# FFN units on inputs that carry the row factor, convolution taps read from PSUM, and 2 KB tiles placed at 0 modulo 128

## The chip, the cores and the metric

The kernel runs on one core of one Trainium2 chip. The metric is the device time of one launch in microseconds (us), the median of three timed runs; lower is better. Beside it stands one profiled execution, whose trace gives every duration below.

## The reference, cut to what matters

Two transformer-like blocks follow each other on 512 tokens of width 1024, in float32. The first ends with a feed-forward layer whose two halves pass through a causal convolution of three taps:

```
h2 = rms_norm(x, ffn_pre_g)                       # row factor r(token) and gain g(channel)
u  = h2 @ w_up                                    # (512, 8192)
c  = conv_w[0]*u[t-2] + conv_w[1]*u[t-1] + conv_w[2]*u[t] + conv_b
g, val = split(c)                                 # 4096 + 4096 columns
x  = x + rms_norm((gelu_tanh(g) * val) @ w_down, ffn_post_g)
```

The second block normalises x again and applies one input projection (query, index, gate, recurrence and merge columns), sparse attention over the 256 best keys, a linear recurrence, and output projections. Before the feed-forward layer the first block has a sliding-window and a differential attention.

## The kernel before, in words

**Layout.** Activations lie transposed: channels on the 128 partitions, 512 tokens along the free axis, so that a tile of 128 channels is 128 x 512 in float32, 2 KB per partition. A 1024-wide activation is eight such tiles (index k). Each is kept twice, as a high part rounded to float32r and the low rest (`xh`, `xl`). Weights are split likewise (`wh`, `wl`, or `sh`, `sl` in two halves when all four places for `wh` are taken). A product is then three matmuls (`mm3`, lines 534 to 546): xh with wh, xl with wh, xh with wl.

**Units.** One unit is 128 output channels: eight k times three matmuls, 24 matmuls of 512 columns into one PSUM buffer. The weights of one unit are 512 KB, fetched by SyncE into one of three `wr` buffers, copied to `wh` by ScalarE (`hi_w`, line 477) and subtracted into `wl` by VectorE or GpSimd (`lo_w`, line 495). `unit` (line 548) runs one unit. `group` (line 561) runs several, with `outer="k"` interleaved: for each k all units of the group. With `halves=True` it does the first 256 tokens of all units, then the others. Behind a unit stands its evacuation, a generator that reads PSUM.

**Order.** No engine's order is fixed by hand. While the program is built, a planner (`account`, line 288; `sched`, line 437; `until`, line 453) keeps a modelled time for each engine and lets a generator go on when its engine and data are ready in that model. What comes out is one fixed order per engine, and each engine works in that order and waits for semaphores. `vp` (line 357) puts a subtraction or product on VectorE or GpSimd, whichever the model has free first.

**PSUM.** Eight buffers of 128 x 512: two each of `mm`, `lg`, `pt`, `o`. `psm` (line 385) takes the buffer of a unit from the kinds in `self.mmt`. In the feed-forward layer that is `("mm",)`, two buffers.

**The boundary between stages** (`boundary`, line 1177) adds the normalised output to the residual `xres`, writes the next stage's `xh`, `xl` with the gain g but without the row factor r (which needs all channels), and computes r into `rbn` (two halves, `nx["rok"]`). So the next stage's matmuls start before r is known, and r is multiplied in when a unit's PSUM is evacuated.

**The feed-forward layer** (`ffn`, line 1219). ug0, uv0, ug1 run as a group in halves. Then uv1, ug2, uv2, ... each run as a unit; after every eight pairs come the eight `dn` units on `acth`, `actl`. The evacuation of an up unit (`conv`, line 1228) is: VectorE `u` = PSUM times r and release of the PSUM buffer; ScalarE `c` = u times tap 2 plus bias; VectorE twice `c` += u shifted by one (511 columns) and by two (510 columns) times a tap. Then ScalarE takes the gelu (gate half), or VectorE or GpSimd the product and ScalarE and VectorE the split into `acth`, `actl` (value half).

**The second block** (`block2`, line 1336) starts with ckv, kw, qi0 in halves and the group qi1, qi2, qi3 on unscaled inputs. Beside that group `rescale` (line 1405) computes, for each k that the group has read (`qk["k"]`), xres times gain times r into `xn` on VectorE, and `resplit` writes it into the same eight places as new `xh`, `xl`. All later units of that block use these (`xs2`), and their evacuation needs no r. `ev_xr` (line 1555) reads its convolution taps from PSUM.

**SBUF.** Pools lie one behind the other in the order in which they are opened (lines 240 to 243): `pers`, `wpool`, `slots`, `small`. `pers` begins at a multiple of 128 bytes and holds first vec (672 columns, 2,688 bytes) and con (4,608 bytes), both whole multiples of 128, then vec0 and ones with 32 bytes each, and behind these xres and the sixteen `xh`, `xl`. So those 2 KB tiles begin at 64 modulo 128. `wpool` (wr, wh, wl) and `slots` (all other 2 KB tiles, such as acth, aoh, hxh, mixh, mxh, sh) begin at 0 modulo 128.

Of the kernel before, what the change touches and what calls it, by code (L numbers as in the profile page):

```python
# [12 lines left out]
F32 = mybir.dt.float32  # L13
F32R = mybir.dt.float32r
AF = mybir.ActivationFunctionType
OP = mybir.AluOpType

P = 128
S = 512
D = 1024  # L20
KT = D // P
# [212 lines left out]
class _Build:  # L234
    def __init__(self, tc, ctx, ins, out, dbg=None):
        self.tc, self.ins, self.out, self.dbg = tc, ins, out, dbg
        self.realnc = tc.nc
        self.nc = _NC(self, tc.nc)
        E = ctx.enter_context
        self.pers = E(tc.tile_pool(name="pers", bufs=1))  # L240
        self.wpool = E(tc.tile_pool(name="wpool", bufs=1))
        self.slots = E(tc.tile_pool(name="slots", bufs=1))
        self.small = E(tc.tile_pool(name="small", bufs=1))
        self.psum = E(tc.tile_pool(name="psum", bufs=1, space=bass.MemoryType.PSUM))
        E(tc.manual_schedule())
        self.W, self.raw, self.hi = {}, {}, {}
        self.n_dma = self.n_hi = self.n_lo = 0
        self.live, self.la, self.cur, self.crit = 0, 3, 0, 0
        self.cnt = 0
        self.active, self.queues = [], []  # L250
        self.T = {}
        self.free = dict(T=0.0, D=0.5, A=0.6, P=0.6, S=-0.5)
        self.wf, self.rf = {}, {}
        self.fam = None
        self.rawrel, self.wrel = {}, [0.0] * NWT
        self.fin, self.issued = 0.0, 0
        LAT.update(T=PRM["LT"], D=PRM["LD"], A=PRM["LA"], P=PRM["LP"], S=3.2)
        self.psn = dict(mm=0, lg=0, pt=0, o=0)
        self.psrel = {k: [0.0, 0.0] for k in self.psn}
        self.mmt, self.nlg = ("mm",), 0  # L260
# [399 lines left out]
    def new_xs(self):  # L660
        out = []
        for k in range(KT):
            out.append((self.pers.tile([P, S], F32R, name=self.nm(f"xh{k}"), tag=f"xh{k}", bufs=1),
                        self.pers.tile([P, S], F32R, name=self.nm(f"xl{k}"), tag=f"xl{k}", bufs=1)))
        return out

    def warm(self, func):
# [46 lines left out]
    def setup(self):  # L714
        nc, ins = self.nc, self.ins
        self.vec = self.pers.tile([P, NV], F32, name="vec")
        self.con = self.pers.tile([P, NCON], F32, name="con")
        self.vec0 = self.pers.tile([P, 8], F32, name="vec0")
        self.ones = self.pers.tile([P, 1], F32, name="ones")
        nc.vector.memset(self.ones, 1.0)  # L720
        self.xres = [self.pers.tile([P, S], F32, name=f"xres{k}") for k in range(KT)]
        self.warm(AF.Sqrt)
        dz = self.slot("dz", F32R)
        nc.vector.tensor_copy(dz, self.ones.to_broadcast([P, S]))
        pz = self.ps("o")
        for _ in range(8):
            self.realnc.tensor.matmul(pz, dz[:, :P], dz, start=True, stop=True)
        self.rel(pz)
        for u in range(3):
            self.raw[u] = self.wpool.tile([P, KT * P], F32, name=f"wr{u}", tag="wr", bufs=NRAW)  # L730
        for n in ("x0", "v", "w00", "x1", "w10", "w20", "x2", "x3", "w01", "x4", "w11", "w21", "x5", "x6", "x7"):
            if n == "v":
                nc.sync.dma_start(self.vec0, ins["vec"][:, 0:8])
            elif n[0] == "x":
                nc.sync.dma_start(self.xres[int(n[1])], ins["xt"][:, int(n[1]), :])
            else:
                u, h = int(n[1]), int(n[2])
                nc.sync.dma_start(self.raw[u][:, h * S:(h + 1) * S], ins["wpk"][u, :, h * S:(h + 1) * S])
        self.n_dma = 3
        nc.sync.dma_start(self.con, ins["con"])  # L740
        nc.sync.dma_start(self.vec, ins["vec"])

        def c(n):
            o, w = COFF[n]
            return self.con[:, o:o + w]
        self.ident, self.tab, self.swa = c("ident"), c("tab"), c("swa")
        self.cmask, self.cdup = c("cmask"), c("cdup")
# [429 lines left out]
    def boundary(self, ys, acc, done, post, pre, dname):  # L1177
# [38 lines left out]
            self.spawn(chain(s), prio=0)  # L1216
        return nx

    def ffn(self, nx):
        nc = self.nc  # L1220
        xs, rb = nx["xs"], nx["rb"]
# [6 lines left out]
        def conv(ps, sl, j):  # L1228
            while not all(nx["rok"][s.start] for s in HALF if sl in (FULL, s)):
                yield  # L1230
            if sl.start == 0:
                U2[j] = self.slot("u")
            u = U2[j]
            yield "D"
            nc.vector.tensor_mul(u[:, sl], ps[:, sl], rb[:, sl])
            self.rel(ps)
            if sl.stop < S:
                return None
            del U2[j]
            yield "A"  # L1240
            c = self.slot("c")
            nc.scalar.activation(c, u, AF.Identity, bias=self.v("cb", j), scale=self.v("cw2", j))
            yield "D"
            nc.vector.scalar_tensor_tensor(c[:, 1:], u[:, :S - 1], self.v("cw1", j), c[:, 1:], op0=OP.mult,
                                           op1=OP.add)
            nc.vector.scalar_tensor_tensor(c[:, 2:], u[:, :S - 2], self.v("cw0", j), c[:, 2:], op0=OP.mult,
                                           op1=OP.add)
            yield "A"
            return c

        def ev_g(j):
            def f(ps, sl):
                c = yield from conv(ps, sl, j)
                if c is None:
                    return
                nc.scalar.activation(c, c, AF.Gelu_apprx_tanh)
                hold[j] = c
            return f

        def ev_u(j):  # L1260
            def f(ps, sl):
                c = yield from conv(ps, sl, 32 + j)
                if c is None:
                    return
                while j not in hold:
                    yield
                yield "E"
                g = hold.pop(j)
                self.vp(S).tensor_mul(c, c, g)
                yield "A"  # L1270
                act[j] = yield from self.split(c, None, name="act")
            return f
# [23 lines left out]
        def drop(g):  # L1296
            for j in range(8 * g, 8 * g + 8):
# [3 lines left out]
                   tags=("mm", "mm", "lg", "lg", "o", "o"), halves=True, outer="k",  # L1301
                   ready=lambda u, k, sl: nx["ok"][sl.start][k])
        self.la = 3
        for g in range(NG):
            for j in range(8 * g, 8 * g + 8):
                if j > 1:
                    self.unit(f"ug{j}", xs, ev_g(j))
                if j > 0:
                    self.unit(f"uv{j}", xs, ev_u(j))
                if j == 8 * g and g >= 1:  # L1310
                    a = need(g - 1)
                    for f in range(8):
                        self.unit(f"dn{g - 1}_{f}", a, ev_d(g - 1, f))
                    a = None
                    drop(g - 1)
        g = NG - 1
        N = [f"dn{g}_{f}" for f in range(8)]
        E = [ev_d(g, f) for f in range(8)]
# [3 lines left out]
        def rd(u, k, sl):  # L1322
            a[k] = act.get(8 * g + k)
            return a[k] is not None
        self.la = PRM["la"]
        self.group(N[:3], a, E[:3], outer="k", late=[6, 7], ready=rd)
        self.drain()
        for f in (3, 4):
# [7 lines left out]
    def block2(self, nx):  # L1336
        nc, T = self.nc, self.T
        xs, rb = nx["xs"], nx["rb"]
        wuk, wuv, wrg, wrt = [], [], [], []
        for n in range(4):  # L1340
            t = self.slot("wrg")
            nc.scalar.dma_start(t, self.ins["wrg"][:, n, :])
            wrt.append(t)
        for n in range(2):
            t = self.slot("wuv")
# [31 lines left out]
        def ev(name, scale=None):  # L1377
            def f(ps, sl):
# [11 lines left out]
                if sl.stop == S:  # L1390
# [9 lines left out]
                   ready=lambda u, k, sl: nx["ok"][sl.start][k])  # L1400
        self.la = 3
        xs2 = [None] * KT
        qk = {"k": -1}

        def rescale():
            while not nx["rok"][256]:
                yield
            for k in range(KT):
                while qk["k"] < k:
                    yield "D"  # L1410
                yield "D"
                t = self.slot("xn")
                nc.vector.scalar_tensor_tensor(t, self.xres[k], self.v("norm2", k), rb, op0=OP.mult, op1=OP.mult)
                self.spawn(resplit(k, t), prio=1, hint="A")

        def resplit(k, t):
            xs2[k] = yield from self.split(t, None, dst=(
                self.pers.tile([P, S], F32R, name=self.nm("xh"), tag=f"xh{k}", bufs=1),
                self.pers.tile([P, S], F32R, name=self.nm("xl"), tag=f"xl{k}", bufs=1)))

        Dt = {0: self.tab[:, 384:512]}
        V = [[None, None] for _ in range(4)]
# [123 lines left out]
        self.spawn(prep())  # L1546
        self.spawn(prep_c())
        self.spawn(topk())
        self.spawn(rescale(), prio=1)
        self.group(["qi1", "qi2", "qi3"], xs, [ev(f"qi{t}", 0.125) for t in (1, 2, 3)], outer="k", note=qk)  # L1550
        xs = None

# [124 lines left out]
        rb = None  # L1677
# [9 lines left out]
        for n in range(2):  # L1687
            t = self.slot("wuk")
# [255 lines left out]
```

## Time and profile before

| what | value |
|---|---|
| median of three timed runs | 1333.4 us (1333.04 to 1334.54) |
| the profiled execution's own time | 1329.96 us |
| its span, first to last instruction | 1328.1 us |
| TensorE matmul busy | 1290.4 us, 97% |
| VectorE, ScalarE, GpSimd busy | 901.3, 708.0, 301.8 us |
| granted TensorE clock, mean | 0.99 |

The span is the time between the first and the last instruction of the trace; the own time of the same execution is 1.9 us longer. The stages by the trace: first block to about 209 us, start of the feed-forward layer 209 to 240, its units to 760, start of the second block to 830, its projections and recurrence to 1020, attention to 1200, the last projections and the output to 1328.

### The profile page before, as it was taken

What the parts mean: (1) busy time and instruction counts of PE and PEld (TensorE: products, weight loads), DVE (VectorE), ACT (ScalarE), POOL (GpSimd) and SP (SyncE); (2) the same over time, 40 slices, a digit from 0 to 9 for tenths busy, and PEclk for the clock granted to TensorE, in tenths of its full rate; (3) what the DMA queues carried; (4) which work ended last, traced back from release to release, by engine and by line L of the source; (5) the groups of instructions that cost most, each with busy time, mean ns of one, the idle gap of its engine ahead of it and who ended that gap; (6) DMA issues with size and microseconds to landing.
All of it is one profiled execution on the core that took longest, in us unless ns stands there. A gap on an engine that the chain in (4) does not pass through costs nothing.

```text
span 1328.1 us, 17863 instructions
## 1 busy us (share of the span) xinstructions
PE 1290.4 (97%) x6748; PEld 1065.6 (80%) x6748; DVE 901.3 (68%) x1586; ACT 708.0 (53%) x1258; POOL 301.8 (23%) x204
## 2 busy tenths in 40 slices
PE   9999998999999999999999988999999999999997
PEld 7788888888888888888887875888788778787886
DVE  6768768776266736674677689588989676753354
ACT  7598765344234313432344455888771778783332
POOL 4301015223034303330333353031220000010111
PEclk9999999999999999999999989999999999999998
DMA  6302240233323332333224410222223121122321
GB/s 234 89 24 64 65 146 30 64 95 96 109 81 95 95 111 80 95 95 107 85 95 132 138 48 16 64 80 79 80 94 114 64 64 48 49 63 96 95 65 64
DMA packets 34245, 113.23 MB, mean 85 GB/s; under 512 B 3824, under 2 KB 5872, under 8 KB 34160
## 3 DMA queue, kind: packets, MB, share of 16 engines
q1 hardware_dynamic: 32192, 109.48, 26.4%
q10 hardware_dynamic: 1968, 2.62, 0.6%
q8 instruction: 53, 0.87, 0.3%
q14 instruction: 32, 0.26, 0.1%
HBM read 109.99 MB, written 2.10 MB: 84 GB/s over the span
## 4 chain that ended last, share of the span: by engine, by line
PE 76%; DVE 16%; ACT 4%; issue 2%; DMA 1%; SPq 0%; POOL 0%; ACTq 0%; DVEq 0%; POOLq 0%
PE ps_mm L214 58%; PE ps_lg L214 8%; PE ps_o L214 8%; DVE c L214 3%; PE ps_pt L214 3%; DVE sq L214 1%; DVE xl L214 1%; DVE sl L214 1%; DVE score L214 1%; ACT wh L214 1%; ACT c L214 1%; DVE wl L214 1%; DVE yo L214 1%; DVE m L214 1%; ACT L214 1%
## 5 line engine op out<-in xcount | busy, mean ns | idle before, releaser
L214 PE MATMUL ps_mm<-xh,wh 128*128 128x512 f32 x840 | 336.8, 401 | 0.0
L214 PE MATMUL ps_mm<-xh,wl 128*128 128x512 f32 x840 | 331.1, 394 | 0.1
L214 PE MATMUL ps_mm<-xl,wh 128*128 128x512 f32 x840 | 330.8, 394 | 0.0
L214 POOL TENSOR_TENSOR wl<-wr,wh 128x1024 fp32r<-128x1024 f32 (+1 forms) x69 | 166.4, 2412 | 423.5 <-ACT wh L214 423.5
L214 ACT ACTIVATE wh<-wr 128x1024 fp32r<-128x1024 f32 (+1 forms) x179 | 185.4, 1038 | 130.9 <-PE ps_mm L214 96.8
L214 DVE SCALAR_TENSOR_TENSOR c<-u,vec,c 128x511 f32<-128x511 f32 (+1 forms) x128 | 171.6, 1342 | 74.8 <-ACT c L214 72.5
L214 PEld LDWEIGHTS ps_mm<-xh,wl 128*128 128x128 f32 x840 | 158.5, 189 | 38.7 <-POOL wl L214 0.8
L214 PEld LDWEIGHTS ps_mm<-xh,wh 128*128 128x128 f32 x840 | 158.7, 189 | 36.5 <-issue 2.0
L214 PEld LDWEIGHTS ps_mm<-xl,wh 128*128 128x128 f32 x840 | 158.8, 189 | 33.6 <-DVE xl L214 0.2
L214 DVE TENSOR_TENSOR wl<-wr,wh 128x1024 fp32r<-128x1024 f32 (+1 forms) x110 | 134.3, 1221 | 72.5 <-ACT wh L214 72.1
L214 ACT ACT_TABLE_LOAD x65 | 83.4, 1283 | 6.0 <-PE ps_mm L214 2.5
L214 PE MATMUL ps_mm<-acth,wh 128*128 128x512 f32 x216 | 84.3, 390 | 2.3 <-DVE fs L214 2.3
L214 PE MATMUL ps_mm<-actl,wh 128*128 128x512 f32 x216 | 84.1, 389 | 0.0
L214 PE MATMUL ps_mm<-acth,wl 128*128 128x512 f32 x216 | 84.1, 389 | 0.0
L214 ACT ACTIVATE acth<-c 128x512 fp32r<-128x512 f32 x32 | 20.2, 632 | 114.0 <-DVE c L214 111.2
L214 ACT ACTIVATE c<-c 128x512 f32<-128x512 f32 x32 | 20.2, 632 | 81.8 <-DVE c L214 81.8
L214 ACT ACTIVATE c<-u,vec 128x512 f32<-128x512 f32 x64 | 51.5, 808 | 13.5 <-DVE u L214 13.5
L214 POOL TENSOR_TENSOR sq<-sq,sq 128x256 f32<-128x256 f32 (+1 forms) x38 | 36.1, 950 | 92.4 <-ACT sq L214 77.9
L214 DVE TENSOR_TENSOR u<-ps_mm,rbn 128x512 f32<-128x512 f32 (+1 forms) x63 | 42.5, 676 | 15.1 <-PE ps_mm L214 15.1
L214 PEld LDWEIGHTS ps_mm<-acth,wh 128*128 128x128 f32 x216 | 40.5, 188 | 11.8 <-DVE fs L214 2.7
L214 POOL MEMSET skl<- 64x512 f32 x28 | 14.7, 526 | 147.4 <-PE ps_pt L214 62.7
L214 PEld LDWEIGHTS ps_mm<-actl,wh 128*128 128x128 f32 x216 | 40.5, 188 | 8.4
(407 smaller groups left out, 2640.9 us busy)
## 6 DMA issues: line engine op xcount, KB each, us to landing
wr<-in_wpk_dram SPq DMA_DIRECT2D x197, 512.0 KB, 3.6
xres<-in_xt_dram SPq DMA_DIRECT2D x8, 256.0 KB, 5.5
wr<-in_wpk_dram SPq DMA_DIRECT2D x6, 256.0 KB, 5.6
wrg<-in_wrg_dram ACTq DMA_DIRECT2D x4, 256.0 KB, 4.2
out_dram<-o SPq DMA_DIRECT2D x4, 256.0 KB, 2.2
out_dram<-o ACTq DMA_DIRECT2D x3, 256.0 KB, 2.2
con<-in_con_dram SPq DMA_DIRECT2D x1, 576.0 KB, 6.1
wuv<-in_wukv_dram ACTq DMA_DIRECT2D x2, 256.0 KB, 5.4
```

Source lines behind the costliest of these rows:

```text
L214: r = f(*a, **k)
```

## The change

Three things are changed. The pool with the large tiles is opened first, so that xres, xh and xl begin at 0 modulo 128. The feed-forward layer gets the second block's `rescale`, now a method: uv1, ug2, uv2 become one group with `outer="k"`, beside which the inputs are scaled; ug3 and uv3 run as a group that waits for each k, and all units from ug3 on read the scaled inputs. Their evacuation (`conv2`) has no `u`: ScalarE and VectorE read PSUM, which is released after the last tap, and units take buffers from `mm`, `o` and `lg` until the last eight dn units. In the diff, what is left out does this: `new_xs`, xres and `resplit` take their tiles from `big`; the second block calls the same `rescale` with its own gain; `ev_g` and `ev_u` use `conv` for j below 3 and `conv2` from j = 3 on; the last line stands ahead of the group of the last dn units.

```diff
+        self.big = E(tc.tile_pool(name="big", bufs=1))
         self.wpool = E(tc.tile_pool(name="wpool", bufs=1))
         self.slots = E(tc.tile_pool(name="slots", bufs=1))
+        self.pers = E(tc.tile_pool(name="pers", bufs=1))
...
+    def rescale(self, nx, pre, xs2, qk):
+        nc = self.nc
+        while not nx["rok"][256]:
+            yield
+        for k in range(KT):
+            while qk["k"] < k:
+                yield "D"
+            yield "D"
+            t = self.slot("xn")
+            nc.vector.scalar_tensor_tensor(t, self.xres[k], self.v(pre, k), nx["rb"], op0=OP.mult, op1=OP.mult)
+            self.spawn(self.resplit(k, t, xs2), prio=1, hint="A")
...
+        def conv2(ps, j):
+            yield "A"
+            c = self.slot("c")
+            nc.scalar.activation(c, ps, AF.Identity, bias=self.v("cb", j), scale=self.v("cw2", j))
+            yield "D"
+            nc.vector.scalar_tensor_tensor(c[:, 1:], ps[:, :S - 1], self.v("cw1", j), c[:, 1:], op0=OP.mult,
+                                           op1=OP.add)
+            nc.vector.scalar_tensor_tensor(c[:, 2:], ps[:, :S - 2], self.v("cw0", j), c[:, 2:], op0=OP.mult,
+                                           op1=OP.add)
+            self.rel(ps)
+            yield "A"
+            return c
...
         self.la = 3
+        xs2 = [None] * KT
+        qk = {"k": -1}
+        self.spawn(self.rescale(nx, "ffn_pre", xs2, qk), prio=1)
+        self.group(["uv1", "ug2", "uv2"], xs, [ev_u(1), ev_g(2), ev_u(2)], outer="k", note=qk)
+        xs = None
+        self.mmt = ("mm", "o", "lg")
+        self.group(["ug3", "uv3"], xs2, [ev_g(3), ev_u(3)], outer="k", ready=lambda u, k, sl: xs2[k] is not None)
         for g in range(NG):
             for j in range(8 * g, 8 * g + 8):
-                if j > 1:
-                    self.unit(f"ug{j}", xs, ev_g(j))
-                if j > 0:
-                    self.unit(f"uv{j}", xs, ev_u(j))
+                if j > 3:
+                    self.unit(f"ug{j}", xs2, ev_g(j))
+                    self.unit(f"uv{j}", xs2, ev_u(j))
...
+        self.mmt = ("mm",)
```

## Rows read from the trace of the kernel before

**Rows 1.** Page, part 1: busy time of each engine.
```profile
PE 1290.4 (97%) x6748; PEld 1065.6 (80%) x6748; DVE 901.3 (68%) x1586; ACT 708.0 (53%) x1258; POOL 301.8 (23%) x204
```
**Rows 2.** Waits of TensorE: waiter, releaser, us in total, times, longest.
```profile
PE ps_pt L214 <- DVE r L214: 5.0, 4, 2.3
PE ps_lg L214 <- ACT csh L214: 4.6, 1, 4.6
...
PE ps_lg L214 <- DVE xl L214: 3.9, 3, 2.2
...
PE ps_mm L214 <- DVE fs L214: 2.3, 1, 2.3
```
**Rows 3.** Windows: length, busy of PE, PEld, DVE, ACT, POOL, then granted clock, DMA.
```profile
240.00:730.00 490.00, 487.66 (x2108) 394.40 (x2107) 303.82 (x307) 182.62 (x235) 141.19 (x61) 1.00 0.31 96
760.00:830.00 70.00, 55.61 (x320) 45.65 (x319) 61.85 (x125) 36.78 (x77) 31.59 (x30) 0.90 0.13 43
830.00:1020.00 190.00, 188.31 (x824) 152.97 (x823) 159.11 (x267) 138.86 (x186) 35.64 (x18) 1.00 0.28 85
1020.00:1200.00 180.00, 180.00 (x1108) 143.46 (x1107) 124.04 (x329) 134.25 (x281) 9.67 (x15) 1.00 0.19 59
```
**Rows 4.** Timeline of PE, a unit on ao, then one on x: start, us, engine.
```profile
1244.76 0.39 PE L214 MATMUL ps_mm<-aoh,wh 128*128 128x512 f32 x1
...
1250.22 0.39 PE L214 MATMUL ps_mm<-xh,wh 128*128 128x512 f32 x1
...
1255.82 0.39 PE L214 MATMUL ps_mm<-aoh,wh 128*128 128x512 f32 x1
```
**Rows 5.** Timeline of PE, up units without a gap: first and last of 130.
```profile
264.75 0.40 PE L214 MATMUL ps_mm<-xh,sh 128*128 128x512 f32 x1
...
294.86 0.39 PE L214 MATMUL ps_mm<-xh,wh 128*128 128x512 f32 x1
```
**Rows 6.** Timeline of PE, dn units without a gap: first and last of 134.
```profile
329.64 0.39 PE L214 MATMUL ps_mm<-acth,wh 128*128 128x512 f32 x1
...
359.78 0.39 PE L214 MATMUL ps_mm<-actl,wh 128*128 128x512 f32 x1
```
**Rows 7.** Timeline of PE, 256 columns: stationary x (six steps), moving xh (eight), acth (fifteen).
```profile
93.93 0.28 PE L214 MATMUL ps_mm<-wh,xh 128*128 128x256 f32 x1
...
94.64 0.28 PE L214 MATMUL ps_mm<-wh,xh 128*128 128x256 f32 x1
...
210.07 0.28 PE L214 MATMUL ps_lg<-xh,wh 128*128 128x256 f32 x1
...
210.98 0.28 PE L214 MATMUL ps_mm<-xh,wl 128*128 128x256 f32 x1
...
740.09 0.28 PE L214 MATMUL ps_mm<-acth,sl 128*128 128x256 f32 x1
...
741.89 0.28 PE L214 MATMUL ps_mm<-acth,sl 128*128 128x256 f32 x1
```
**Rows 8.** Groups by shape, evacuation of up units: busy, mean ns, idle before.
```profile
L214 DVE SCALAR_TENSOR_TENSOR c<-u,vec,c 128x511 f32<-128x511 f32 x64 | 121.7, 1902 | 72.5 <-ACT c L214 72.5
...
L214 DVE SCALAR_TENSOR_TENSOR c<-u,vec,c 128x510 f32<-128x510 f32 x64 | 50.0, 782 | 2.3
L214 DVE TENSOR_TENSOR u<-ps_mm,rbn 128x512 f32<-128x512 f32 x61 | 41.8, 685 | 15.1 <-PE ps_mm L214 15.1
```
**Rows 9.** Tile xrc, taps from PSUM in block 2: ns min/median/max, starts.
```profile
L214 DVE SCALAR_TENSOR_TENSOR xrc<-ps_o,vec,xrc x15: 735/742/750, 833.7 to 957.0; 128x511 f32<-128x511 f32 x5, 128x510 f32<-128x510 f32 x5, 128x509 f32<-128x509 f32 x5
...
L214 ACT ACTIVATE xrc<-ps_mm,vec x3: 772/781/798, 871.7 to 948.3; 128x512 f32<-128x512 f32 x3
```
**Rows 10.** Tile xn, the scaling in block 2: ns min/median/max, starts.
```profile
L214 DVE SCALAR_TENSOR_TENSOR xn<-xres,vec,rbn x8: 721/744/1741, 794.4 to 812.9; 128x512 f32<-128x512 f32 x8
L214 ACT ACTIVATE xh<-xn x8: 614/632/633, 795.2 to 813.8; 128x512 fp32r<-128x512 f32 x8
...
L214 DVE TENSOR_TENSOR xl<-xn,xh x3: 678/691/692, 803.5 to 806.5; 128x512 fp32r<-128x512 f32 x3
```

More of the change, by code (lines that the diff above doesn't have):

```diff
@@ L239, in __init__ @@
         E = ctx.enter_context
-        self.pers = E(tc.tile_pool(name="pers", bufs=1))
+        self.big = E(tc.tile_pool(name="big", bufs=1))
         self.wpool = E(tc.tile_pool(name="wpool", bufs=1))
         self.slots = E(tc.tile_pool(name="slots", bufs=1))
+        self.pers = E(tc.tile_pool(name="pers", bufs=1))
         self.small = E(tc.tile_pool(name="small", bufs=1))
@@ L662, in new_xs @@
         for k in range(KT):
-            out.append((self.pers.tile([P, S], F32R, name=self.nm(f"xh{k}"), tag=f"xh{k}", bufs=1),
-                        self.pers.tile([P, S], F32R, name=self.nm(f"xl{k}"), tag=f"xl{k}", bufs=1)))
+            out.append((self.big.tile([P, S], F32R, name=self.nm(f"xh{k}"), tag=f"xh{k}", bufs=1),
+                        self.big.tile([P, S], F32R, name=self.nm(f"xl{k}"), tag=f"xl{k}", bufs=1)))
         return out
@@ L720, in setup @@
         nc.vector.memset(self.ones, 1.0)
-        self.xres = [self.pers.tile([P, S], F32, name=f"xres{k}") for k in range(KT)]
+        self.xres = [self.big.tile([P, S], F32, name=f"xres{k}") for k in range(KT)]
         self.warm(AF.Sqrt)
@@ L1217, in boundary, with resplit @@
         return nx
+    def rescale(self, nx, pre, xs2, qk):
[9 more added lines that the diff above has]
+            self.spawn(self.resplit(k, t, xs2), prio=1, hint="A")
+    def resplit(self, k, t, xs2):
+        xs2[k] = yield from self.split(t, None, dst=(
+            self.big.tile([P, S], F32R, name=self.nm("xh"), tag=f"xh{k}", bufs=1),
+            self.big.tile([P, S], F32R, name=self.nm("xl"), tag=f"xl{k}", bufs=1)))
     def ffn(self, nx):
@@ L1249, in conv @@
             return c
+        def conv2(ps, j):
[10 more added lines that the diff above has]
+            return c
         def ev_g(j):
             def f(ps, sl):
-                c = yield from conv(ps, sl, j)
+                c = yield from (conv(ps, sl, j) if j < 3 else conv2(ps, j))
                 if c is None:
@@ L1261, in f @@
             def f(ps, sl):
-                c = yield from conv(ps, sl, 32 + j)
+                c = yield from (conv(ps, sl, 32 + j) if j < 3 else conv2(ps, 32 + j))
                 if c is None:
@@ L1403, in block2 @@
         qk = {"k": -1}
[L1405 to L1419, printed above, removed]
         Dt = {0: self.tab[:, 384:512]}
@@ L1548, in block2 @@
         self.spawn(topk())
-        self.spawn(rescale(), prio=1)
+        self.spawn(self.rescale(nx, "norm2", xs2, qk), prio=1)
         self.group(["qi1", "qi2", "qi3"], xs, [ev(f"qi{t}", 0.125) for t in (1, 2, 3)], outer="k", note=qk)
```

## The prediction

> **What bounds the kernel now.** I read the page's busy times first: PE's matmuls are busy 97% of the span, VectorE 68%, ScalarE 53% [rows 1]. Busy matmuls overlap, so I looked next at what TensorE waits for. The waits are few: 5.0 us on the row factor, 4.6 on csh, 3.9 on xl, 2.3 on fs, and twelve smaller kinds, some 31 us in all of 1328 [rows 2]. [...] Inside the feed-forward units there is one wait, the 2.3 us on fs near the end.
>
> Fourth, the spacing, from the timeline. Units that stream xh and xl: 264.75 to 294.86 us over 129 steps, 0.2334 us a matmul of 512 columns [rows 5]. Units that stream acth and actl: 329.64 to 359.78 over 133 steps, 0.2266 us [rows 6]. Same shape, same weights, same clock. It is not the stretch of the program either: where units on ao and on x take turns, the 24 matmuls on aoh and aol take 5.46 us and the 24 on xh and xl behind them 5.60 [rows 4]. What tells the two kinds apart in the program is their place: xh and xl begin at 64 modulo 128, everything in `slots` at 0. All tiles at 64 lie in one region as well, so the trace cannot part the two.
>
> **The sum, part by part**, against the profiled execution (own time 1329.96 us, span 1328.1; the median of the timed runs is 1333.4, 3.4 above it, and I carry differences over to the median as they are).
>
> *Placement.* Full-width units on xh and xl: 14 in block 1 (ka, qa, va, kb, qb), 61 up units, 51 in block 2 (three qi, eight each of xr, gr, mr, q, ga, ma), 126 units of 24, 3024 matmuls. At 0 modulo 128 I take the spacing of rows 6: 3024 x (0.2334 - 0.2266) = 3024 x 0.0068 = -20.5 us. The bounds are 0, if place is not the cause, and -20.5: no row at 512 columns is faster than 0.2266.
>
> Not all of it reaches the end. ka, qa0, qa1 run while inputs arrive, and qi1 to qi3, xr0, xr1 run beside the chain that leads to the 4.6 us wait on csh: a faster TensorE there only waits longer. That is eight units, 192 matmuls, +1.3 us.
>
> Matmuls of 256 columns show no such gain. Moving xh at 64: 0.91 us over eight steps, 0.114; moving acth at 0: 1.80 over fifteen, 0.120; moving wh with x stationary: 0.71 over six, 0.118 [rows 7]. If acth's 0.120 goes with place 0, the two groups in halves (288 matmuls) lose at most 288 x 0.006 = 1.7 us and the two vb pairs (192) 192 x 0.002 = 0.4; the other end is -288 x 0.004 = -1.2, if 0.114 should come where 0.118 stands now. Much of the halves waits for the boundary anyway. I take +1.0.
>
> *Scaled inputs from ug3 on.* Added: eight xn at 0.744 us on VectorE, eight xh at 0.632 on ScalarE, eight xl at 0.691 if on VectorE [rows 10]: 11.5 us of VectorE, 5.1 of ScalarE. They lie beside the group uv1, ug2, uv2, which takes 72 x 0.2266 = 16.3 us, so a k is free every 2.04 us. After the last k one xh and one xl follow, 1.3 us; the next group reads that k seven steps of six matmuls later, 9.5 us. VectorE also has the first three evacuations there, three times 0.685 + 1.902 + 0.782 = 10.1 us [rows 8], in all 21.6 us in 16.3 + 9.5 = 25.8, so it fits, with weight subtractions and some xl on GpSimd, but not by much. Block 2 has the same handover, and none of its PE waits names an xl of `resplit` at xr0: the waits on xl are in the halves [rows 2]. The bounds are 0 and the 4.6 us that the same place of block 2 does lose to its longest chain. Nearest to the cost is the handover without a wait: I take +0.7. The weights of all three units must be there within nine matmuls; the planner prepares them at the boundary with a look-ahead of six units, so I charge nothing.
>
> *Evacuation from PSUM.* Per unit u goes (0.685 us), the 511-column tap falls from 1.902 to the 0.742 of xrc, the other from 0.782 to 0.742, ScalarE's c takes 0.78 (0.81 before) [rows 8, 9]. For 58 units that is 58 x (0.685 + 1.160 + 0.040) = 109 us off VectorE, which is busy 304 of 490 us [rows 3]. TensorE doesn't wait for it now, so on the path it is worth nothing. What changes is the hold on a PSUM buffer: from one VectorE step to c and two taps, 0.78 + 2 x 0.74 = 2.3 us plus queueing. With two buffers the next unit but one would need it after 5.4 us; with six, after five units, 27 us. At the last dn group the kinds are mm, mm, lg again, and if ug31 and uv31 sit on both mm buffers, the group starts up to 2.3 us late; or the wait on fs behind it goes, -2.3. I take 0.
>
> *Order.* The planner makes a new order from 237 us on. Block 2's code is the same, but its 4.6 us wait can go or come twice: 0, ends -4.6 and +4.6.
>
> Sum: -20.5 + 1.3 + 1.0 + 0.7 = -17.5 us, an own time of 1312.5 in a profiled execution, and 1333.4 - 17.5 = 1315.9 for the median; I say 1316.
>
> [...]
>
> **The rivals.** *Part of it is given back.* VectorE is busy 159 of 190 us in projections and recurrence [rows 3], and a faster TensorE leaves every other engine 3% less time per unit. Two more waits of csh's size, 9.2 us, give 1325. For it: the order is planned anew and a wait costs clock besides (0.90 granted at the start of block 2). Against it: stretches on acth already run at 0.2266 without a wait. Chance 0.13, times 1322 to 1330.
>
> *Place is not the cause* (the region, or something in how x is written). Then the spacing stays 0.2334, and the handover's 0.7 stands alone: 1334. For it: all tiles at 64 modulo 128 lie together, and xh at 256 columns runs at 0.114, the fast rate per column, from the same place. Against it: aoh and acth lie all over a pool of 104 KB and show one spacing, and xh shows its own whether sh or wh is stationary [rows 4 to 6]. Chance 0.09.
>
> *Slower: the evacuation holds TensorE at each up unit.* ScalarE's c now reads PSUM ahead of the weight copies in the same queue, VectorE's taps stand behind c, and behind those the weight subtractions that TensorE needs. It decides from 17.5/58 = 0.30 us per unit. If every second unit came late by what the 511-column tap now loses, 1.16 us [rows 8, 9], that is 58 x 0.58 = 33.6 us: 1349. For it: three units are evacuated at once before ug3, and the first two groups depend on that queue. Against: 27 us of cover, and VectorE has 109 us less to do. Chance 0.06.
>
> **How the numbers follow.** The forecast has the remaining 0.72, with its own range 1308 to 1322 (-4.6 and the halves' -2.2 below, handover +3.9 and dn group +2.3 above). A measurement of this kernel tells 0.2%, 2.7 us, from no change. Faster: 0.72 + 0.13 = 0.85. Same: 0.08, nearly all of the second rival. Slower: 0.07, the third and what the second can lose to order. The range for 8 in 10 takes in the forecast's and most of the first rival's: 1308 to 1327.
>
> **What would show it.** Right: starts of xh matmuls 0.2266 to 0.227 apart in all stages, while acth stays; no waits inside 255 to 700 us; VectorE near 200 us in the feed-forward window; taps at 0.74. Wrong: xh still at 0.233 (place is not the cause); a PE wait on xl or xh at ug3 (handover); waits on VectorE's c or on wl in each up unit (third rival); more than 10 us of new waits after 760 (first rival).

## The result, and the profile after

The changed kernel takes 1316.1 us (median of four runs, 1314.47 to 1316.57); the kernel before, run beside it, 1333.2 (1330.35 to 1334.54). The ratio is 0.9874, with a 95% interval of 0.9859 to 0.9889. The forecast was 1316.0. The time was right. The reasons were right in part: as the experiments show, placement alone brings 4 us and not 17, and the lighter evacuation, priced at nothing, is what lets it bring more. The profiled execution has a span of 1312.7 us and an own time of 1314.5, against 1328.1 and 1329.96 before.

First the page's busy times, the answer to [rows 1]:
```profile
PE 1272.3 (97%) x6748; PEld 1064.4 (81%) x6748; DVE 865.5 (66%) x1592; ACT 713.3 (54%) x1266; POOL 185.5 (14%) x156
```
TensorE has the same 6748 matmuls and is busy 18 us less. VectorE lost only 36 us, GpSimd 116.

Next TensorE's waits, the answer to [rows 2] (waiter, releaser, us in total, times, longest):
```profile
PE ps_pt L214 <- DVE r L214: 6.6, 5, 2.5
PE ps_lg L214 <- ACT csh L214: 4.7, 1, 4.7
PE ps_lg L214 <- DVE xl L214: 4.5, 3, 2.1
...
PE ps_mm L214 <- ACT xh L214: 3.2, 2, 3.0
PE ps_lg L214 <- ACT xch L214: 2.3, 1, 2.3
```
The wait on csh stayed, as forecast for a chain that TensorE does not set. The wait on fs is gone, and one on xch is now 2.3 us.

The windows, the answer to [rows 3]:
```profile
240.00:730.00 490.00, 490.00 (x2180) 406.40 (x2179) 275.85 (x324) 195.53 (x256) 27.98 (x17) 1.00 0.32 99
760.00:830.00 70.00, 58.78 (x313) 47.15 (x314) 60.37 (x112) 39.44 (x74) 27.70 (x23) 0.93 0.15 46
830.00:1020.00 190.00, 187.02 (x823) 153.85 (x823) 159.74 (x280) 132.79 (x176) 34.06 (x18) 0.99 0.28 86
1020.00:1200.00 180.00, 180.00 (x1113) 144.55 (x1112) 118.90 (x308) 135.57 (x282) 10.10 (x14) 1.00 0.19 59
```
In the feed-forward window TensorE does 2180 matmuls where it did 2108, and is busy for all of the 490 us. VectorE falls there from 303.82 to 275.85 us and GpSimd from 141.19 to 27.98: the planner gave VectorE nearly all of GpSimd's weight subtractions (85 `wl` on VectorE where it did 27, 2 on GpSimd where it did 56), which take about half as long there (1.22 us against 2.40). The prediction had named 200 us for VectorE among its signs of being right; the 109 us of evacuation did go, but those 58 subtractions bring back 71.

The timeline of TensorE, up units without a gap (the first and last of 277 matmuls) and, above, the first group in halves (twelve steps of 256 columns), the answer to [rows 5, 7]:
```profile
209.32 0.28 PE L214 MATMUL ps_mm<-xh,sh 128*128 128x256 f32 x1
...
210.76 0.28 PE L214 MATMUL ps_mm<-xh,wh 128*128 128x256 f32 x1
...
255.06 0.39 PE L214 MATMUL ps_o<-xh,sl 128*128 128x512 f32 x1
...
317.62 0.39 PE L214 MATMUL ps_lg<-xh,wl 128*128 128x512 f32 x1
```
62.56 us over 276 steps is 0.2267 us a matmul, acth's pace of [rows 6], where it was 0.2334. The halves run at 0.120, where xh ran at 0.114.

Last the tiles c and xn, the answer to [rows 8 to 10] (duration min/median/max in ns):
```profile
L214 DVE SCALAR_TENSOR_TENSOR c<-ps_mm,vec,c x42: 748/749/751, 280.7 to 700.5; 128x511 f32<-128x511 f32 x21, 128x510 f32<-128x510 f32 x21
...
L214 DVE TENSOR_TENSOR c<-c,c x29: 681/685/1787, 274.8 to 702.2; 128x512 f32<-128x512 f32 x29
...
L214 DVE SCALAR_TENSOR_TENSOR c<-u,vec,c x12: 735/750/1665, 241.7 to 267.3; 128x511 f32<-128x511 f32 x6, 128x510 f32<-128x510 f32 x6
```
A tap from PSUM takes 0.749 us at 511 and at 510 columns. The old kind, c<-u, has a maximum of 1665 ns beside a median of 750. The 1.9 us of [rows 8] belong to what ran beside the tap, not to 511 columns (last section).

Where the time went, by milestones in the traces (the first matmul of a kind, or the last), in us per stage. "x off" are the experiments e3, e4 and e7 below, which have the whole change except the distance of x from the weights:

| stage | before | after | x off |
|---|---|---|---|
| halves and r (209 to 237) | 27.87 | 25.99 | 26.2 to 27.5 |
| feed-forward units | 520.50 | 508.43 | 517.5 to 518.3 |
| start of block 2, to the first matmul on csh | 68.73 | 68.65 | 68.7 to 68.8 |
| projections and recurrence | 154.58 | 155.27 | 155.1 to 155.3 |
| matmuls on hx | 43.33 | 43.52 | 43.3 to 43.6 |
| attention | 176.11 | 174.78 | 175.8 to 176.1 |
| last projections | 127.65 | 126.72 | 127.4 to 127.9 |

Block 1 takes 209.4 us before and 209.3 after, and 209.5 to 212.6 in the experiments up to e9. Its code is the same in most of these, so 3 us of a difference between two executions can be of that kind, and stages tell more than sums.

### The profile page after: what moved, and what is told of

It reads as the page before. It is cut to its first block, busy times and chain, and to the rows that moved or that the text cites. A ratio compares the mean times of both kernels' runs of the same rounds, so it can differ in the third digit from the quotient of the medians.

```text
span 1312.7 us, 17705 instructions
## 1 busy us (share of the span) xinstructions
PE 1272.3 (97%) x6748; PEld 1064.4 (81%) x6748; DVE 865.5 (66%) x1592; ACT 713.3 (54%) x1266; POOL 185.5 (14%) x156
## 4 chain that ended last, share of the span: by engine, by line
PE 81%; DVE 12%; ACT 3%; issue 2%; DMA 0%; SPq 0%; POOL 0%; DVEq 0%; ACTq 0%; POOLq 0%
PE ps_mm L214 40%; PE ps_lg L214 20%; PE ps_o L214 19%; PE ps_pt L214 3%; DVE xl L214 1%; DVE score L214 1%; DVE sq L214 1%; DVE wl L214 1%; DVE fs L214 1%; ACT L214 1%; DVE sl L214 1%; DVE yo L214 1%; DVE m L214 1%; DVE g L214 0%; DMA xres<-in_xt_dram 0%
## 5 line engine op out<-in xcount | busy, mean ns | idle before, releaser
L214 DVE TENSOR_TENSOR wl<-wr,wh 128x1024 fp32r<-128x1024 f32 (+1 forms) x164 | 200.0, 1220 | 73.6 <-ACT wh L214 73.2
L214 PE MATMUL ps_mm<-xh,wh 128*128 128x512 f32 (+1 forms) x568 | 226.8, 399 | 0.7 <-ACT wh L214 0.4
L214 PE MATMUL ps_mm<-xl,wh 128*128 128x512 f32 (+1 forms) x568 | 221.4, 390 | 0.3 <-DVE xl L214 0.3
L214 PE MATMUL ps_mm<-xh,wl 128*128 128x512 f32 (+1 forms) x568 | 221.0, 389 | 0.6 <-POOL wl L214 0.6
L214 PE MATMUL ps_o<-xh,wh 128*128 128x512 f32 (+1 forms) x256 | 97.1, 379 | 0.0
L214 PE MATMUL ps_o<-xl,wh 128*128 128x512 f32 (+1 forms) x256 | 96.5, 377 | 0.0
L214 PE MATMUL ps_o<-xh,wl 128*128 128x512 f32 (+1 forms) x256 | 96.4, 377 | 0.0
L214 PE MATMUL ps_lg<-xh,wh 128*128 128x512 f32 (+1 forms) x168 | 63.9, 381 | 0.0
L214 PE MATMUL ps_lg<-xl,wh 128*128 128x512 f32 (+1 forms) x168 | 63.9, 381 | 0.0
L214 PE MATMUL ps_lg<-xh,wl 128*128 128x512 f32 (+1 forms) x168 | 63.9, 380 | 0.0
```

Of the source, the lines that this page charges most:

```text
L214: r = f(*a, **k)
```

## The experiments

In all of e2 to e9 but e5, every engine does the same operations on the same tiles in the same order as in the kernel that the edit starts from (apart from the memsets of the pads, and from which PSUM buffer a unit uses). So the planner's order has no part in these comparisons. In e5, 15 instructions stand in another place, between 259 and 277 us; e10 is planned anew.

**e1: the matmul alone.** A kernel of nothing but float32r matmuls, with moving and stationary tiles at chosen places, 30 matmuls a series without a break.

```diff
+MOV = [("mzero", 0), ("mthirty", 32), ("msixty", 64), ("mninety", 96)]
+STA = [("wzero", 0), ("wthirty", 32), ("wsixty", 64), ("wninety", 96)]
+    for wn in ("wzero", "wsixty"):
+        for mn in ("mzero", "mthirty", "msixty", "mninety"):
+            series("full", wn, mn)
...
+    for mn in ("mplus", "mtwo"):
+        series("full", "wzero", mn)
```


> This kernel computes nothing of the reference: it runs series of float32r matmuls alone, with the start of the moving and of the stationary tile at 0, 32, 64 or 96 modulo 128, with 512 and 256 columns, with one and three PSUM buffers, and with four small float32 transposes put in after every 3, 6, 12 or 24 matmuls. Theory (place of the moving tile): 512 columns at 0 run 0.2266 us apart, at 64 0.2334, with either stationary tile; tiles further on by 128 and 256 run as at 0. If the relative place counts, both at 64 run at 0.2266 and stationary at 64 with moving at 0 at 0.2334. If the region or the writing of x is the cause, all series run alike. For the interleaved series, theory from the changed kernel's trace: after a transposition the next matmuls run at 0.228 to 0.236 wherever the tile is, so that place 0 gains 0.007 us a matmul only from runs of more than some twelve matmuls on; rival: the gain is 0.007 in every series. 256 columns: 0.120 at 0, 0.114 to 0.118 at 64.

The series follow each other without a gap, so the first matmul of each (timeline of TensorE; mplus lies 128 bytes and mtwo 256 further from wzero than mzero does) gives 30 steps:
```profile
17.79 0.39 PE L246 MATMUL full<-mzero,wzero 128*128 128x512 f32 x1
...
24.59 0.40 PE L246 MATMUL full<-mthirty,wzero 128*128 128x512 f32 x1
...
31.59 0.39 PE L246 MATMUL full<-msixty,wzero 128*128 128x512 f32 x1
...
38.46 0.40 PE L246 MATMUL full<-mninety,wzero 128*128 128x512 f32 x1
...
45.47 0.39 PE L246 MATMUL full<-mzero,wsixty 128*128 128x512 f32 x1
...
52.47 0.40 PE L246 MATMUL full<-mthirty,wsixty 128*128 128x512 f32 x1
...
59.46 0.39 PE L246 MATMUL full<-msixty,wsixty 128*128 128x512 f32 x1
...
66.28 0.40 PE L246 MATMUL full<-mninety,wsixty 128*128 128x512 f32 x1
...
101.30 0.39 PE L246 MATMUL full<-mplus,wzero 128*128 128x512 f32 x1
...
108.27 0.39 PE L246 MATMUL full<-mtwo,wzero 128*128 128x512 f32 x1
...
115.09 0.39 PE L246 MATMUL bank<-mzero,wzero 128*128 128x512 f32 x1
```
The first number is the place of the moving tile, the second that of the stationary one. 0 with 0: 6.80 us over 30 steps, 0.2267. 32 with 0: 7.00, 0.2333. 64 with 0: 6.87, 0.2290. 0 with 64: 7.00, 0.2333. 64 with 64: 6.82, 0.2273, and once settled 0.2267. At a distance of 128 (mplus) 6.97, 0.2323; at 256 (mtwo) 6.82 again. So place does set the pace, but as the distance between the moving and the stationary tile modulo 256 bytes; "0 modulo 128" is neither needed nor enough. Why the distance counts, no run shows.

Further series put four small f32 transposes between groups of matmuls. The mean spacing inside the groups, at place 0 and at 64: groups of 3, 0.2706 and 0.2748; of 6, 0.2484 and 0.2488; of 12, 0.2372 and 0.2375; of 24, 0.2313 and 0.2330. In groups of six or twelve little is left. But the weights lie at 0 here, where 64 costs only 0.0022 us in a long series; the x of the kernel before has the pace of 0 with 64, 0.0066 slower. So these series show that short groups lose gain, and not how much of it the kernel loses. At 256 columns the series settle at 0.1200 (0 with 0), 0.1178 (64 with 0) and 0.1133 (0 with 64).

**e2: place alone.** The kernel before, with xres, xh and xl in a pool opened first.

```diff
-        self.pers = E(tc.tile_pool(name="pers", bufs=1))
+        self.big = E(tc.tile_pool(name="big", bufs=1))
         self.wpool = E(tc.tile_pool(name="wpool", bufs=1))
         self.slots = E(tc.tile_pool(name="slots", bufs=1))
+        self.pers = E(tc.tile_pool(name="pers", bufs=1))
...
```


> The kernel before with the large tiles in a pool that is opened first, nothing else changed; the order of instructions is that of before. Theory (place is the cause of nearly all): 14 to 16 us faster than before, 1317 to 1319, with xh matmuls 0.2267 apart in the feed-forward layer and the wait of 2.3 us on fs still there. Rival (the feed-forward edits bring a good part): less than 10 us faster.

1328.4 us (1326.63 to 1330.45), ratio 0.9970 (0.9959 to 0.9982): only 4 us. Matmuls on xh are 0.2267 apart here too, but the feed-forward units take 519.1 us. The waits of TensorE between 237 and 760 us, two of them in its timeline, and the window behind the last:
```profile
PE ps_mm L214 <- DVE fs L214: 4.7, 3, 3.5
PE ps_mm L214 <- DVE u L214: 2.5, 5, 0.5
```
```profile
441.63 0.39 PE L214 MATMUL ps_mm<-xh,wl 128*128 128x512 f32 x1
442.52 0.47 PE L214 MATMUL ps_mm<-xh,wh 128*128 128x512 f32 x1 [0.50 <-DVE u L214]
...
725.04 0.39 PE L214 MATMUL ps_lg<-acth,wl 128*128 128x512 f32 x1
728.95 0.80 PE L214 MATMUL ps_mm<-acth,wh 128*128 128x512 f32 x1 [3.52 <-DVE fs L214]
```
```profile
729.00:732.00 3.00, 3.00 (x8) 2.38 (x9) 1.94 (x4) 2.22 (x7) 0.83 (x2) 0.53 0.55 175
```
Seven steps like that at 441.63 (0.83 to 1.12 us where 0.23 was due) cost 4.8 us together, and the step behind each 0.08 more; five of them wait for u and two for fs. 725.04 to 728.95 costs 3.7, and the seven steps behind it, at a granted clock of 0.53 (here called the half level: 0.43 us a matmul), cost 1.5. Together that is all but 0.2 of the 10.7 us by which the feed-forward units take longer than in the changed kernel. TensorE has become fast enough to catch up with the evacuation.

**e3: the feed-forward edits alone.** The changed kernel, with the pools in the old order (x at 64).

```diff
-        self.big = E(tc.tile_pool(name="big", bufs=1))
+        self.pers = self.big = E(tc.tile_pool(name="pers", bufs=1))
...
-        self.pers = E(tc.tile_pool(name="pers", bufs=1))
```


> The changed kernel with all its large tiles back in the first pool behind vec, con, vec0 and ones, at 64 modulo 128; scaled inputs, taps from PSUM and six buffers stay. Theory: 0 to 4 us faster than before (1329 to 1333), by the wait on fs near the end of the feed-forward layer that the changed kernel no longer has; xh matmuls at 0.2333. Rival: 8 us or more faster, then the place is not all of it; second rival, slower than before by the handover.

1328.7 us (1326.45 to 1329.18), ratio 0.9971 (0.9960 to 0.9982): 3.6 us. Matmuls on xh stay 0.2333 apart (278 matmuls from 255.23 to 319.86), the wait on fs is gone, TensorE is busy 490.00 of 490 us. 4 and 3.6 us alone, 16 to 17 together: the two parts need each other.

**e4: another region, the old place.** The changed kernel with 64 bytes ahead of the x tiles and 64 behind.

```diff
+        pada = self.big.tile([P, 16], F32, name="pada")
...
         self.xres = [self.big.tile([P, S], F32, name=f"xres{k}") for k in range(KT)]
...
+        padb = self.big.tile([P, 16], F32, name="padb")
...
```


> The changed kernel with 64 bytes put ahead of xres and 64 behind xh and xl: those tiles are at 64 modulo 128 again, in the new region, and all others at 0. Theory (place modulo 128): as the kernel without the move, 1329 to 1333, xh matmuls at 0.2333. Rival (the region of SBUF): as the changed kernel, 1316, xh matmuls at 0.2267.

1328.3 us (1326.62 to 1330.66), ratio 0.9972 (0.9962 to 0.9982), xh at 0.2333 (278 matmuls, 255.14 to 319.77). So the region is not the cause.

**e5: two buffers.** The changed kernel, its up units on `mm` alone.

```diff
-        self.mmt = ("mm", "o", "lg")
+        self.mmt = ("mm",)
         self.group(["ug3", "uv3"], xs2, ...)
```


> The changed kernel, but up units from ug3 on take their PSUM buffers from mm alone (two buffers instead of six). In the run with place alone TensorE lost 4.7 us to seven waits of 0.6 to 0.9 us on VectorE's u (two buffers, old evacuation) and 4.7 us to fs. Theory 'evacuation': what took those waits away is the lighter VectorE work (no u, taps of 0.74 us, a hold of 2.3 us on a buffer), not the number of buffers; then 1315 to 1318 us, units of the feed-forward layer 508 to 511 us long, no wait of TensorE on c or ps in 240 to 730 us. Theory 'buffers': six buffers carry it; then waits on VectorE's c come in that stretch, 5 us or more in all, and the time is 1321 to 1328.

1328.5 us (1326.1 to 1331.37), ratio 0.9977 (0.9963 to 0.9991). TensorE's waits from 237 to 760 us, and two windows:
```profile
PE ps_mm L214 <- ACT xh L214: 4.4, 1, 4.4
PE ps_mm L214 <- DVE c L214: 3.5, 1, 3.5
```
```profile
255.00:265.00 10.00, 5.65 (x18) 4.18 (x17) 9.93 (x11) 5.85 (x8) 5.37 (x4) 0.83 0.00 0
...
275.00:290.00 15.00, 13.75 (x54) 11.25 (x55) 7.08 (x10) 5.74 (x9) 1.53 (x1) 0.89 0.24 71
```
The size is near that of the theory "buffers" (1328.5, just above its range), the place is not: two waits at the handover to the scaled inputs, where VectorE (third of the busy times) works 9.93 of 10 us, and a granted clock of 0.83 and 0.89 behind them. After that there is no wait up to the end of the units.

**e6: place and six buffers, the old evacuation.** e2, with the up units from uv1 on in `mm`, `o` and `lg`.

```diff
+        self.mmt = ("mm", "o", "lg")
         for g in range(NG):
...
+        self.mmt = ("mm",)
         self.group(N[:3], a, E[:3], outer="k", late=[6, 7], ready=rd)
```


> The kernel before with the 2 KB tiles at 0 modulo 128 (as in the run with place alone, 1328.4) and six PSUM buffers for up units from uv1 on, but the old evacuation (u, then taps on c in SBUF) and unscaled inputs. Theory 'buffers': the seven waits on u (4.7 us) go, and the wait on fs falls too: 1318 to 1323 us, units 510 to 514 us long. Theory 'evacuation': VectorE's work is what is late, so that a buffer more only moves the wait on (to c, fs or weights): 1325 to 1330, units 517 us or more.

1322.9 us (1320.94 to 1324.4), ratio 0.9934 (0.9912 to 0.9955), units 514.7 us. The waits from 237 to 760 us:
```profile
PE ps_mm L214 <- DVE fs L214: 3.5, 1, 3.5
PE ps_mm L214 <- ACT xh L214: 3.0, 1, 3.0
```
The waits on u are gone, as "buffers" said; one of 0.6 us on c is left, and the one on fs stays. With the steps behind it, that one costs 5.3 of the 6.3 us by which these units still take longer than in the changed kernel. (The 3.0 on xh is the start of block 2, which all kernels have.)

**e7 and e8: distance or 0 modulo 128.** The changed kernel with 128 bytes ahead of x and 128 behind (e7), and with 64 bytes ahead of everything (e8).

```diff
+        pada = self.big.tile([P, 32], F32, name="pada")    # e7; [P, 16] in e8
...
         self.xres = [self.big.tile([P, S], F32, name=f"xres{k}") for k in range(KT)]
...
+        padb = self.big.tile([P, 32], F32, name="padb")    # e7 only
```


> The changed kernel with 128 bytes ahead of xres, xh, xl and 128 behind, so that all large tiles still begin at 0 modulo 128, but x lies 128 modulo 256 away from the weights. Theory 'distance' (the series alone on TensorE: .2267 us where moving and stationary tile have the same place modulo 256, .2329 at a distance of 128): xh matmuls .233 apart, 1326 to 1330 us like the run with x at 64. Theory '0 modulo 128' (the prediction's wording): .2267 and 1315 to 1318 us.

> The changed kernel with 64 bytes ahead of xres, so that every large tile, weights and activations alike, begins at 64 modulo 128 and none at 0. Theory 'distance': xh and acth matmuls .2267 apart as in the changed kernel, 1314 to 1318 us. Theory '0 modulo 128': all 512-column matmuls at .229 to .233, also those on acth: 1326 to 1345 us.

e7: 1328.7 us (1325.84 to 1329.33), ratio 0.9972 (0.9959 to 0.9986). e8: 1315.7 us (1314.67 to 1316.81), ratio 0.9881 (0.9861 to 0.9900). The timelines of TensorE, first and last of 280 matmuls in e7 and of 287 in e8:
```profile
255.13 0.40 PE L214 MATMUL ps_lg<-xh,sl 128*128 128x512 f32 x1
...
319.96 0.39 PE L214 MATMUL ps_lg<-xh,wl 128*128 128x512 f32 x1
```
```profile
255.15 0.39 PE L214 MATMUL ps_lg<-xl,sh 128*128 128x512 f32 x1
...
319.97 0.39 PE L214 MATMUL ps_lg<-xh,wl 128*128 128x512 f32 x1
```
64.83/279 = 0.2324 with every large tile at 0 modulo 128, 64.82/286 = 0.2266 with none there. The distance decides, and "0 modulo 128", in the title and in the prediction, is not what counts.

**e9: six buffers only at the handover.** The changed kernel, back on `mm` from ug4 on.

```diff
         self.group(["ug3", "uv3"], xs2, ...)
+        self.mmt = ("mm",)
```


> The changed kernel, but six PSUM buffers only for the group ug3, uv3; from ug4 on up units use mm alone. With two buffers all through, TensorE waited 4.4 us on xh and 3.5 us on c between 255 and 276 us, at this group, and never again in the up units. Theory 'handover' (the six buffers matter only there, and the light evacuation needs no more than two afterwards): no wait at ug3, 1315 to 1318 us, units 508 to 511 us long. Theory 'steady' (the two-buffer kernel was free of waits later only because it was already late): waits on c come back somewhere in 280 to 740 us, 1319 to 1326 us.

1325.4 us (1321.69 to 1328.08), ratio 0.9941 (0.9919 to 0.9962). TensorE's timeline at its one long wait:
```profile
277.40 0.39 PE L214 MATMUL ps_mm<-xh,wl 128*128 128x512 f32 x1
282.68 0.77 PE L214 MATMUL ps_mm<-xh,wh 128*128 128x512 f32 x1 [4.88 <-DVE c L214]
283.24 0.63 PE L214 MATMUL ps_mm<-xl,wh 128*128 128x512 f32 x1
283.67 0.63 PE L214 MATMUL ps_mm<-xh,wl 128*128 128x512 f32 x1
```
Neither theory has it whole. The wait moved from ug3 to 277 us, just behind the handover; from 283 us on the two buffers suffice, as in e5 (the first dn group to the last, 425.9 us here and in the changed kernel). The matmuls behind the wait come 0.43 us apart, the pace of e2's half level (granted clock 0.77 in the mean of 275 to 290 us), so that it costs more than its 4.9 us: from the first full unit to the first dn unit 89.9 us, where the changed kernel takes 82.5.

**e10: measured matmul costs for the planner.**

```diff
-                c = max(n / 2400.0, 0.1) + 0.003
+                c = max(n / 2400.0, 0.1) + 0.0134
```


> The changed kernel, planned with matmul costs as measured: n/2400 + 0.0134 us for a float32r matmul (0.2267 at 512 columns, 0.120 at 256) in the planner's account, in place of n/2400 + 0.003. Nothing else is changed, but the order of every engine comes out anew. Theory 'a better model orders better': the waits on csh (4.7 us), xch (2.3) and sq shrink, 1309 to 1314 us. Theory 'the parameters suit the short cost' (look-ahead and leads were set with it): waits move, 1314 to 1322 us.

1333.5 us (1329.76 to 1335.56), ratio 1.0004 (0.9992 to 1.0016): 17 us slower than the changed kernel, worse than either theory. TensorE's waits in the whole span:
```profile
PE ps_pt L214 <- DVE sq L214: 9.5, 4, 4.2
PE ps_lg L214 <- DVE xcl L214: 7.5, 2, 4.2
...
PE ps_pt L214 <- DVE vat L214: 3.1, 1, 3.1
```
Block 1 loses 11 us, the halves 7, block 2 4; the feed-forward units (507.8 us) nothing. A truer cost made a worse order. That the leads and look-aheads were set along with the old cost is the likely reason, and was not tried.

## Why the prediction came out right

*Placement* (-20.5, less 1.3 and 1.0): that the place of x sets the pace is right; which place, and the size, are not. What counts is the distance from the weights modulo 256. e7 has every large tile at 0 modulo 128, as the prediction asks, and is as slow as e4. That the changed kernel's x came to lie at distance 0 and not at 128 is luck: the prediction's rule does not tell the two apart. By the table, x at the weights' place gives 9 to 10 us in the feed-forward units, 1.0 to 1.3 in attention and 0.7 to 1.1 in the last projections, 11 to 12 in all; by the medians it is 12.2 to 12.6 (e4, e3 and e7 against the changed kernel). Missing against the sum:

- Projections and recurrence, 22 units, 3.6 us by the sum: nothing. The spacing of xh did fall there (mean of the undisturbed steps 0.2332 before, 0.2274 after), but the stage lasts 154.2 to 155.3 us in all ten kernels up to e9, at either pace. A faster TensorE waits longer for xch (2.3 us, 1.5 before) and takes the eight steps behind that wait at the half level, 1.7 us more (0.43 us a matmul, granted clock 0.57 from 946 to 950 us; before, 0.23 us and 1.00 from 961 to 965 us, behind the same wait). That is the rival "part of it is given back", on a smaller scale, and the windows show it: 187.02 of 190 us busy, 188.31 before.
- Attention, 19 units, 3.1 us by the sum: 1.3. Those matmuls stand among small ones, mostly in groups of 3, 6 or 9, and the timelines of before and after show what a group gains: nothing in its first two steps (0.28 and 0.232 us in both), 0.003 us a step in the third to fifth, and 0.006 from the eighth on.
- Block 1, 11 units, 1.8 us by the sum: nothing to be seen, within a scatter of 3 us, though xh matmuls came closer there too (0.234 to 0.227).

The start of block 2, whose five full-width units the sum had left out as bound by a chain, lasts 68.6 to 68.8 us in eight of the ten kernels, at either pace (71.1 and 71.2 in e5 and e9).

*Evacuation from PSUM* (109 us off VectorE, "on the path it is worth nothing"): this is the step that failed. It was read from a trace in which TensorE took 0.2334 us a matmul, and holds there (e3). At 0.2267 the old evacuation with two buffers is late: e2 loses 5.3 us at seven steps that wait for u or fs, and 5.1 at the last wait on fs. The sum credited placement alone with a gain that needs these edits. The cover had to be worked out at the new pace: it was so only for the new evacuation. That the light evacuation takes the steady waits away with two buffers is shown by e5 and e9, that six buffers do it as well by e6. Which part of the light evacuation does it (no u, taps from PSUM, or a GpSimd that no longer works beside the taps) was not tried.

The other end, "the wait on fs behind it goes, -2.3", was named and valued at 0. It did go: 2.3 us before, 3.5 in e2 and in e6, all with the old evacuation, and none in the changed kernel or in any of the seven experiments with the new one. At the old pace it cost 2.5 us, at the new one 5 with the steps behind it (e2, at a granted clock of 0.53, and e6). Which step of the new evacuation takes it away was not isolated.

*Scaled inputs from ug3 on* (+0.7, 0 to 4.6): 0, TensorE is busy all the time from 240 to 730 us. But that hung on the six buffers. With two, the stretch from the first full unit to the first dn unit is 11.6 us longer, 7.9 of it waits (e5); with six for one group only, 7.4 us, 4.9 of it waits (e9). It is the mechanism of the slower rival, the evacuations queued before ug3, once and not at every unit.

*Halves*: 0.120 us as assumed, and it fits the distance. With 256 columns e1 has 0.113 for 0 with 64, 0.118 for 64 with 0 and 0.120 at equal places; the kernel before has 0.114 where xh streams over weights, 0.118 where wh streams over x, and 0.120 where acth streams over weights [rows 7]. The stage's 1.9 us of gain is not the change's: it scatters from 26.0 to 27.9 us, and e9, which differs from the changed kernel only from ug4 on, has 27.5.

*Order* (0, ±4.6): too narrow. e10 moved 17 us by the order alone; the changed kernel's new order lost nothing that the table shows, and the prediction could not know that.

So -17.5 was forecast. In the profiled execution it is -15.5: 9 to 10 from placement in the feed-forward units, 2.5 from fs, 1.9 from the halves' scatter, 2.2 from attention and the last projections, +0.7 in projections, the rest within 0.2 each. Placement was credited with some 7 us too much, and the fs wait, a free handover and scatter made up most of it. So the time came out right in part by luck. The rival "place is not the cause" fell with e1, e4 and e8.

Of the "twelve smaller kinds" of waits, two are larger than the 2.3 us on fs: sq with 4.4 and xh with 3.1. The sum uses neither.

## What to carry to other kernels

When a change makes the busiest engine faster, work out every cover again at the new pace: a buffer count or an evacuation that costs nothing now may be what the gain depends on, and two edits may each give a quarter of what they give together. Price a faster matmul stage by stage, and only where such matmuls follow each other in long rows (the first two steps of a group in attention gained nothing here) and no other chain sets the stage's length. For float32r matmuls of 512 columns, lay the moving and the stationary tile at the same place modulo 256 bytes of a partition (0.2267 us in e1, 0.229 to 0.234 at the other distances tried), and read the spacing from the timeline; at 256 columns another place was faster in e1 (0.1133 against 0.1200).

## What the runs showed of the hardware

- The spacing of float32r matmuls of 512 columns went with the distance of the two tiles modulo 256: 0.2267 us at 0, 0.229 to 0.234 at the others tried (e1; in the whole kernel 0.2266 at 0 in e8, 0.2333 in e4, 0.2324 in e7). At 256 columns it was not the equal place that was fastest: 0.1200 there, 0.1133 with the moving tile at 0 and the stationary one at 64 (e1).
- The first of a group of matmuls behind four small transposes was followed by the next after 0.31 to 0.32 us, with the moving tile at 0 and at 64 (e1).
- The taps that read SBUF alone were longer where GpSimd worked beside them, those that read PSUM were not. In the kernel before, the 57 taps of 511 columns on u that overlap a GpSimd instruction take 2043 ns in the mean, the seven others 747; of xrc's taps from PSUM, eleven overlap one and take 743 ns, thirteen don't and take 740. So the 1.9 us of a tap was not its length. In the changed kernel GpSimd hardly works there (3 of the 116 taps from PSUM overlap it), so its short taps don't tell whether reading PSUM or the idle GpSimd made them so. In the kernel before, the 56 taps on u that a weight subtraction on GpSimd overlaps end 0.54 to 0.55 us after that subtraction, every one. What holds them until then, no trace shows.
